# A third seven-product pair in an FFN input product, with its buffers, orders and jobs rearranged

## The chip, the cores and the metric

The kernel runs on one core of a Trainium2 chip. The metric is the device time of one execution in microseconds (us), the median of several runs. The engines of the core run side by side, each through its own queue in program order, and wait for each other by semaphores: TensorE (PE; its weight loads are PEld), VectorE (DVE), ScalarE (ACT), GpSimd (POOL) and SyncE (SP, which issues the DMAs).

## What is computed

A decoder trunk of two layers on 256 positions of width 2048, in float32. Each layer has a token mixer (layer 0: causal pooling with a 512x512 map per channel group; layer 1: sparse attention with an indexer), cross-attention to a memory of 256 rows with 4 heads, and a SwiGLU feed-forward network (FFN) of hidden width 5632, each on an RMS-normed input and added to x. A last RMSNorm follows.

```python
for i in range(DEPTH):
    h = rms_norm(x, norm_mix[i])
    x = x + (pool_mixer(h, ...) if i % 2 == 0 else dsa_attention(h, ...))
    x = x + memory_cross_attention(rms_norm(x, norm_xattn[i]), memn, ...)
    x = x + swiglu(rms_norm(x, norm_ffn[i]), ffn_w_in[i], ffn_w_out[i])
def swiglu(h, w_in, w_out):
    g, u = jnp.split(h @ w_in, 2, axis=-1)
    return (jax.nn.silu(g) * u) @ w_out
```

## The kernel before, in words

Every weight is read once, as a *piece* of 128 partitions x 2048 columns (1 MB), by a DMA of SyncE into one of three *raw* buffers. The products run in a reduced float format (fp32r), so each operand is split into a high part and a low rest, and one product is three matmuls of 512 columns: high x high, high x low, low x high. `high` (L151) is a copy on ACT, `low` (L154) a subtraction on DVE, `raw - high`. A plain piece is split in two *units* of 1024 columns (L157). High and low parts lie in buffers of a pool with tag "w": eight tiles of 2048 columns, two per plain piece.

The order on each engine is the order in which the program text issues the instructions, written by hand. `hook` (L243) is called after every few matmuls: it runs one due *job* (a function put aside with a delay in hooks), and issues one unit of splitting for a piece ahead, two where the lead is short. `split_unit` (L201) issues nothing where the tiles held, `state["held"]`, would pass `W_BUFS`. A piece's tiles are given back, in issue order, by `w_done` (L224); on the chip ACT then waits until TensorE's last matmul on that buffer is over.

The FFN's input product works on *chunks* `j` of 512 hidden columns, gate and up, eleven per layer (`chunk_in`, L725). Four accumulators of one PSUM bank each (2 halves of the rows x gate and up) are filled over eight *pairs* `kp` of k-tiles, one piece each. A plain pair takes eight products of 24 matmuls (`eight`). For the pairs in `SEVEN = (3, 5)`, taken as 2x2 blocks, seven products suffice, 21 matmuls (`seven`, L745): four are added to accumulators or intermediate sums `m` (two "sm" and two "tp" PSUM banks), and sums of weight blocks and of activation blocks are needed. The weight sums are made by DVE in `split_seven` (L169), in four steps s0 to s3; s0 fills the first pair of tiles (b), s1 to s3 the second (t). b is given back in the middle of the pair. The activation sums are made by `combine` (L371), called from the second of the two jobs that transpose and split a quarter of x (`Normed.chunk`, L442). When the last seven pair is over, DVE turns `m` into four parts (L777 to L782); at the chunk's end it adds the accumulators to them (L793), ACT and DVE apply silu and the product, and two jobs transpose the result ("spread", L799).

The chunks stand in groups: 0 to 4, then the output product ("fo") of hidden chunks 0 to 3; 5 to 8 and fo of 4 to 7; 9 and 10 and fo of 8 to 10. fo uses two of the same four accumulators for each of four output quarters. `tables` (L854) makes the rotary tables for layer 1; it stands between layer 0's cross-attention and its FFN.

The joint from cross-attention to FFN: each quarter `n` of x is finished by two adds on DVE (`add_to_x`, L472), and jobs then transpose it on TensorE and split it on ACT and DVE (L358, L360).

Of the kernel before, what the change touches and what calls it, by code (L numbers as in the profile page):

```python
# [12 lines left out]
F32 = mybir.dt.float32  # L13
# [7 lines left out]
P = 128  # L21
# [11 lines left out]
SEVEN = (3, 5)  # L33
# [19 lines left out]
RAW_BUFS, W_BUFS, BIG_BUFS, TMP_BUFS = 3, 8, 11, 7  # L53
# [3 lines left out]
def trunk_kernel(ctx: ExitStack, tc: tile.TileContext, a: dict, out: bass.AP):  # L57
# [73 lines left out]
    state = {"load": 0, "split": 0, "cur": 0, "hook": 0, "held": 0}  # L131
# [25 lines left out]
    def split_plain(i, t, w):  # L157

        def unit(c, first):
            def fn():  # L160
                if first:
                    parts[i] = (w_tile("wh"), w_tile("wl"))
# [3 lines left out]
            return 2 if first else 0, fn  # L166
        return [unit(slice(c, min(c + UNIT, w)), c == 0) for c in range(0, w, UNIT)]

    def split_seven(i, t):  # L169

        r = t.rearrange("p (s c) -> p s c", s=4)
        p = {}

        def s0():
            p["bh"], p["bl"] = w_tile("bh"), w_tile("bl")
            p["t"] = wpool.tile([P, 2, 512], F32, tag="t13", name="t13", bufs=1)
            parts[i] = p
            V.tensor_tensor(p["t"], r[:, 2:4, :], r[:, 0:1, :].to_broadcast([P, 2, 512]), op=ALU.add)
# [12 lines left out]

        def s3():
            low(p["tl"][:, 1024:2048], t[:, 0:1024], p["th"][:, 1024:2048])

        return [(2, s0), (2, s1), (0, s2), (0, s3)]

    def is_seven(i):
        key = pieces[i][0]
        return key[0] == "fi" and key[3] in SEVEN

    def split_unit(must=False):  # L201

        i = state["split"]
        if i >= len(pieces):
            return
        load_to(i + RAW_BUFS)
        if not steps:
            steps.extend(split_seven(i, raws[i][0]) if is_seven(i) else split_plain(i, *raws[i]))
        if state["held"] + steps[0][0] > W_BUFS:
            assert not must  # L210
            return
        steps.popleft()[1]()
        if not steps:
            raws.pop(i)
            state["split"] += 1
# [8 lines left out]
    def w_done(tiles=2):  # L224
        parts.pop(state["cur"])
        state["cur"] += 1
        state["held"] -= tiles
# [143 lines left out]
    def combine(tp, kt0, gi):  # L371

        s = work.tile([P, 1024], F32R, tag="sums", name="sums", bufs=2)
        f, c = tmp(), tmp()
        for u in range(2):
            A.activation(f[:, u * S:(u + 1) * S], tp[:, u * S:(u + 1) * S], AF.Copy, scale=gain(gi, kt0 + u))
        a11, a21, a12, a22 = (f[:, i * P:(i + 1) * P] for i in range(4))
# [56 lines left out]
    class Normed:  # L434
# [7 lines left out]
        def chunk(self, n, later=0):  # L442

            def pair(u):
# [4 lines left out]
                if kt0 // 2 in self.seven:  # L449
                    self.sums[kt0 // 2] = combine(tp, kt0, self.gi)  # L450
                sumsq(self.ss[:, u, n:n + 1], x[:, u, n * 512:(n + 1) * 512])

            job(lambda: pair(0), NORM_CHUNK[0] + later)
# [263 lines left out]
    def ffn(L, xn, nxt):  # L717
# [7 lines left out]
        def chunk_in(j):  # L725
# [6 lines left out]
            def eight(kp, w):  # L732
                wh, wl = w
                xt = xn(kp // 2)
                for f, t in ((0, 0), (0, 1), (1, 0), (1, 1)):
                    for u in range(2):
                        k = 2 * (kp % 2) + u
                        ws = c(((2, 0), (1, 3))[u][f])
# [6 lines left out]
            def seven(kp, w):  # L745
# [8 lines left out]
                last = kp == SEVEN[-1]  # L754
# [9 lines left out]
                three(acc[1], *s_(0), bh[:, c(2)], bl[:, c(2)], False, False)  # L764
# [3 lines left out]
                state["held"] -= 2  # L768
                three(acc[2], *a_(1, 1), w["th"][:, c(3)], w["tl"][:, c(3)], False, False)
                hook()  # L770
                for i, (p, si) in enumerate(((5, 2), (7, 3), (6, 1))):
                    three(m[p], *s_(si), w["th"][:, c(i)], w["tl"][:, c(i)], first, last)
                    if i == 1:
                        hook()
                w_done(2)
# [78 lines left out]
    def tables():  # L854
        posf = small.tile([P, 2], F32, tag="posf", name="posf")
        V.tensor_copy(posf, pos)
        ang, kk = (tmp(384).rearrange("p (c t f) -> p c t f", c=2, t=2) for _ in range(2))
# [14 lines left out]
        A.activation(kf, af, AF.Sin)  # L872
        sn, cs = kk[:, 0], kk[:, 1]
# [308 lines left out]
```

## Time and profile before

| | |
|---|---|
| time, three runs | 2001.17, 2001.29, 2003.45 us; median 2001.29 |
| profiled execution | 2002.29 us, its span 2000.5 us |
| mean granted TensorE clock | 0.993 of full |
| busy in the span | PE 1964.8, PEld 1630.6, DVE 1396.4, ACT 976.8, POOL 50.7 us |
| HBM read | 368.45 MB, 185 GB/s over the span |

The span is the time from the first to the last instruction; the execution's own time has some 1.8 us around it. Busy time is the time in which an engine worked. Matmuls overlap, so the time of one matmul in a stream is read from start to start and not from its duration. In the timeline, "x4" merges neighbours of the same kind into one line, and the brackets at the end give the idle time of the engine before the line and what ended it. L12 is line 12 of the kernel.

### The profile page before, as it was taken

To read this page: it belongs to the slowest core of one execution; us is meant where nothing else is said; L and a number is where in the kernel's file an instruction comes from. 1 tells how busy PE (TensorE), PEld (TensorE's weight loads), DVE (VectorE), ACT (ScalarE), POOL (GpSimd) and SP (SyncE) were. 2 spreads that over 40 slices of the span, in tenths; PEclk is the share of its full clock that TensorE was granted. 3 is DMA by queue.
4 is the path that set the end of the run, shared out by engine and by line. 5 is a ranking of instruction groups with operands and counts; after the bars stand their busy time and mean duration, and the time that the engine had idled before them with its cause. 6 is when DMAs were issued, how large, how long until landed. Compare 5 with 4: busy or idle time off the path is not lost.

```text
span 2000.5 us, 23131 instructions
## 1 busy us (share of the span) xinstructions
PE 1964.8 (98%) x9030; PEld 1630.6 (82%) x9030; DVE 1396.4 (70%) x1861; ACT 976.8 (49%) x1286; POOL 50.7 (3%) x97
## 2 busy tenths in 40 slices
PE   8999899999999999999999999899999999999997
PEld 7788788888888888888788888788888888888886
DVE  5765887874687756766777655778875578855774
ACT  6554654453454533544445554655553355533552
POOL 1200200000000000001000000100000000000000
PEclk9999999999999999999999999999999999999999
DMA  9445454565554554554444354355555455554552
GB/s 358 163 148 177 160 211 168 191 217 200 182 204 185 203 197 157 209 212 172 168 148 166 129 185 152 127 210 210 211 189 189 169 197 212 205 191 177 197 210 85
DMA packets 53679, 372.06 MB, mean 186 GB/s; under 512 B 6336, under 2 KB 6976, under 8 KB 9536
## 3 DMA queue, kind: packets, MB, share of 16 engines
q1 hardware_dynamic: 53136, 370.00, 51.3%
q8 instruction: 71, 1.16, 0.2%
q10 hardware_dynamic: 432, 0.57, 0.1%
q14 instruction: 40, 0.33, 0.0%
HBM read 368.45 MB, written 2.10 MB: 185 GB/s over the span
## 4 chain that ended last, share of the span: by engine, by line
PE 93%; DVE 2%; DMA 2%; ACT 1%; issue 1%; POOL 0%; ACTq 0%; DVEq 0%
PE acc L721 13%; PE acc L723 13%; PE acc L722 13%; PE acc L392 13%; PE acc L390 13%; PE acc L391 13%; PE acc L415 2%; PE acc L416 1%; PE tp L722 1%; PE sm L722 1%; PE tp L723 1%; PE sm L721 1%; PE tp L721 1%; PE sm L723 1%; PE tp L806 1%; DMA raw<-in_xv 1%
## 5 line engine op out<-in xcount | busy, mean ns | idle before, releaser
L155 DVE TENSOR_TENSOR wl<-raw,wh 128x1024 fp32r<-128x1024 f32 x600 | 708.0, 1217 | 318.8 <-ACT wh L152 317.5
L152 ACT ACTIVATE wh<-raw 128x1024 fp32r<-128x1024 f32 x600 | 604.6, 1048 | 501.6 <-PE acc L391 268.9
L390 PE MATMUL acc<-wh,big 128*128 128x512 f32 (+1 forms) x1184 | 476.5, 402 | 0.0
L392 PE MATMUL acc<-wh,big 128*128 128x512 f32 (+1 forms) x1184 | 460.2, 389 | 0.0
L391 PE MATMUL acc<-wl,big 128*128 128x512 f32 (+1 forms) x1184 | 459.3, 388 | 0.0
L721 PE MATMUL acc<-wh,big 128*128 128x512 f32 x1056 | 415.2, 393 | 0.0
L723 PE MATMUL acc<-wh,big 128*128 128x512 f32 x1056 | 412.0, 390 | 0.0
L722 PE MATMUL acc<-wl,big 128*128 128x512 f32 x1056 | 411.8, 390 | 0.0
L392 PEld LDWEIGHTS acc<-wh,big 128*128 128x128 f32 x1184 | 222.5, 188 | 46.4
L391 PEld LDWEIGHTS acc<-wl,big 128*128 128x128 f32 x1184 | 223.1, 188 | 43.6 <-issue 1.9
L390 PEld LDWEIGHTS acc<-wh,big 128*128 128x128 f32 x1184 | 222.8, 188 | 43.2 <-issue 1.9
L723 PEld LDWEIGHTS acc<-wh,big 128*128 128x128 f32 x1056 | 198.7, 188 | 41.6
L722 PEld LDWEIGHTS acc<-wl,big 128*128 128x128 f32 x1056 | 199.0, 188 | 40.2
L721 PEld LDWEIGHTS acc<-wh,big 128*128 128x128 f32 x1056 | 198.9, 188 | 40.2
L155 DVE TENSOR_TENSOR bl<-raw,bh 128x1536 fp32r<-128x1536 f32 x44 | 77.2, 1754 | 49.8 <-ACT bh L152 49.8
L152 ACT ACTIVATE bh<-raw 128x1536 fp32r<-128x1536 f32 x44 | 65.5, 1489 | 87.2 <-issue 68.6
L415 PE MATMUL acc<-big,wh 128*128 128x512 f32 x256 | 97.9, 421 | 5.3 <-ACT wh L152 4.6
L472 DVE TENSOR_TENSOR x<-acc,x 128x512 f32<-128x512 f32 x70 | 47.4, 690 | 46.2 <-PE acc L392 46.2
L351 ACT ACTIVATE big<-tp 128x512 fp32r<-128x512 f32 x44 | 26.4, 600 | 101.2 <-PE tp L806 101.2
L416 PE MATMUL acc<-big,wl 128*128 128x256 f32 x256 | 73.0, 285 | 0.5 <-DVE wl L155 0.5
L152 ACT ACTIVATE th<-raw 128x1024 fp32r<-128x1024 f32 x44 | 46.7, 1060 | 39.7 <-DVE raw L186 39.7
L415 PEld LDWEIGHTS acc<-big,wh 128*128 128x128 f32 x256 | 49.5, 193 | 18.2 <-ACT wh L152 4.9
(206 smaller groups left out, 1851.3 us busy)
## 6 DMA issues: line engine op xcount, KB each, us to landing
raw<-in_fi SPq DMA_DIRECT2D x176, 1024.0 KB, 4.8
raw<-in_fo SPq DMA_DIRECT2D x88, 1024.0 KB, 4.8
raw<-in_wq SPq DMA_DIRECT2D x16, 1024.0 KB, 4.8
raw<-in_wao SPq DMA_DIRECT2D x16, 1024.0 KB, 4.9
raw<-in_xv SPq DMA_DIRECT2D x8, 1024.0 KB, 7.0
raw<-in_xq SPq DMA_DIRECT2D x8, 1024.0 KB, 4.8
raw<-in_xo SPq DMA_DIRECT2D x8, 1024.0 KB, 4.8
raw<-in_wqi SPq DMA_DIRECT2D x8, 1024.0 KB, 5.0
```

The source lines that it names most:

```text
L152: A.activation(dst, src, AF.Copy)
L155: V.tensor_tensor(dst, src, hi.bitcast(F32), op=ALU.subtract)
L351: A.activation(dst_h, src, AF.Copy)
L390: T.matmul(acc[:, :w], lhsT=xh, rhs=wh[:, c0:c0 + w], start=first, stop=False)
L391: T.matmul(acc[:, :w], lhsT=xh, rhs=wl[:, c0:c0 + w], start=False, stop=False)
L392: T.matmul(acc[:, :w], lhsT=xl, rhs=wh[:, c0:c0 + w], start=False, stop=last)
L415: T.matmul(acc, lhsT=wh[:, c0:c0 + P], rhs=xt[:, k, :], start=first, stop=False)
L416: T.matmul(acc[:, S:2 * S], lhsT=wl[:, c0:c0 + P], rhs=xt[:, k, 0:S], start=False, stop=last)
L472: V.tensor_tensor(xc, acc[t], xc, op=ALU.add)
L721: T.matmul(acc, lhsT=xh, rhs=wh, start=first, stop=False)
L722: T.matmul(acc, lhsT=xh, rhs=wl, start=False, stop=False)
L723: T.matmul(acc, lhsT=xl, rhs=wh, start=False, stop=last)
```

## The change

The seven-product set becomes (1, 3, 5) in chunks 1 to 10 of each layer; chunk 0 keeps (3, 5). The pairs are taken in another order, 0, 2, 1, 4, 3, 6, 5, 7 (chunk 0: 0, 1, 2, 4, 3, 6, 5, 7), so that a plain pair stands between any two seven pairs and one plain pair behind the last. High and low parts share one buffer: four of twice the size in place of eight. The four weight blocks lie in another order in memory, and `split_seven` makes the sums in place in the raw buffer, without a tile of its own. Outside `chunk_in` the splitting may hold three buffers only (`W_SHORT`), inside it four. In `Normed.chunk` the scaled copies for the activation sums are made in the transposing job (`scaled`), and the sums themselves in a job of their own, one hook later. The rotary tables become two jobs in the first output product of layer 0.

```diff
-SEVEN = (3, 5)
+PAIRS, SEVEN = (0, 2, 1, 4, 3, 6, 5, 7), (1, 3, 5)
+PAIRS_FIRST, SEVEN_FIRST = (0, 1, 2, 4, 3, 6, 5, 7), (3, 5)
...
-RAW_BUFS, W_BUFS, BIG_BUFS, TMP_BUFS = 3, 8, 11, 7
+RAW_BUFS, W_BUFS, BIG_BUFS, TMP_BUFS = 3, 4, 11, 7
+W_SHORT = 3
...
-            for kp in range(8):
+            for kp in (PAIRS if j else PAIRS_FIRST):
                 plan(("fi", L, j, kp), a["fi"][L, j, kp])
...
-        return wpool.tile([P, 2048], F32R, tag="w", name=name, bufs=W_BUFS)
+        return wpool.tile([P, 2, 2048], F32R, tag="w", name=name, bufs=W_BUFS)
...
         def s0():
-            p["bh"], p["bl"] = w_tile("bh"), w_tile("bl")
-            p["t"] = wpool.tile([P, 2, 512], F32, tag="t13", name="t13", bufs=1)
+            b = w_tile("b")
+            p["bh"], p["bl"] = b[:, 0, :], b[:, 1, :]
             parts[i] = p
-            V.tensor_tensor(p["t"], r[:, 2:4, :], r[:, 0:1, :].to_broadcast([P, 2, 512]), op=ALU.add)
-            high(p["bh"][:, 0:1536], t[:, 512:2048])
-            low(p["bl"][:, 0:1536], t[:, 512:2048], p["bh"][:, 0:1536])
+            for c in (slice(0, 1024), slice(1536, 2048)):
+                high(p["bh"][:, c], t[:, c])
+                low(p["bl"][:, c], t[:, c], p["bh"][:, c])
 
         def s1():
-            p["th"], p["tl"] = w_tile("th"), w_tile("tl")
-            high(p["th"][:, 0:1024], p["t"].rearrange("p s c -> p (s c)"))
-            V.tensor_tensor(r[:, 0, :], p["t"][:, 0, :], r[:, 3, :], op=ALU.add)
-            V.tensor_tensor(r[:, 1, :], r[:, 0, :], r[:, 1, :], op=ALU.add)
+            b = w_tile("t")
+            p["th"], p["tl"] = b[:, 0, :], b[:, 1, :]
+            V.tensor_tensor(r[:, 1:3, :], r[:, 1:4:2, :], r[:, 2:3, :].to_broadcast([P, 2, 512]), op=ALU.add)
+            high(p["th"][:, 512:1536], t[:, 512:1536])
+            V.tensor_tensor(r[:, 3, :], r[:, 1, :], r[:, 3, :], op=ALU.add)
+            V.tensor_tensor(r[:, 0, :], r[:, 3, :], r[:, 0, :], op=ALU.add)
 
         def s2():
-            high(p["th"][:, 1024:2048], t[:, 0:1024])
-            low(p["tl"][:, 0:1024], p["t"].rearrange("p s c -> p (s c)"), p["th"][:, 0:1024])
+            for c in (slice(1536, 2048), slice(0, 512)):
+                high(p["th"][:, c], t[:, c])
+            low(p["tl"][:, 512:1536], t[:, 512:1536], p["th"][:, 512:1536])
 
         def s3():
-            low(p["tl"][:, 1024:2048], t[:, 0:1024], p["th"][:, 1024:2048])
-        return [(2, s0), (2, s1), (0, s2), (0, s3)]
+            for c in (slice(1536, 2048), slice(0, 512)):
+                low(p["tl"][:, c], t[:, c], p["th"][:, c])
+        return [(1, s0), (1, s1), (0, s2), (0, s3)]
...
-        if state["held"] + steps[0][0] > W_BUFS:
+        if state["held"] + steps[0][0] > (W_BUFS if must else state["cap"]):
...
                 if kt0 // 2 in self.seven:
-                    self.sums[kt0 // 2] = combine(tp, kt0, self.gi)
+                    f = scaled(tp, kt0, self.gi)
+                    late.append(lambda: self.sums.update({kt0 // 2: combine(f)}))
...
+            if {2 * n, 2 * n + 1} & set(self.seven):
+                job(sums, NORM_CHUNK[1] + 1 + later)
...
+            pairs, sevens = (PAIRS, SEVEN) if j else (PAIRS_FIRST, SEVEN_FIRST)
+            for kp in pairs:
...
+            state["cap"] = W_BUFS
             for j in range(t0 + (gi > 0), t1 + (not last)):
                 chunk_in(j)
+            state["cap"] = W_SHORT
+            for fn in between if gi == 0 else ():
+                job(fn, 6)
...
-    tables()
-    ffn(0, f0, m1)
+    ffn(0, f0, m1, tables())
```

## Rows read from the trace of the kernel before

**Rows 1.** The page, part 1: busy time of each engine

```profile
PE 1964.8 (98%) x9030; PEld 1630.6 (82%) x9030; DVE 1396.4 (70%) x1861; ACT 976.8 (49%) x1286; POOL 50.7 (3%) x97
```

**Rows 2.** Stages, one FFN chunk: stretch, length, busy PE, PEld, DVE, ACT, POOL, clock

```profile
297.48:340.57 43.09, 43.09 (x195) 35.70 (x194) 34.56 (x36) 22.09 (x23) 0.00 (x0) 1.00 0.54 195
```

**Rows 3.** TensorE's waits: who ended them; us in total, times, longest

```profile
PE tp L367 <- DVE x L472: 12.4, 2, 6.2
...
PE tp L585 <- DVE big L360: 3.2, 1, 3.2
...
PE tp L512 <- DVE tmp L506: 2.0, 1, 2.0
```

**Rows 4.** Timeline of TensorE, one chunk: start us, us, engine, line, operation

```profile
309.30 0.39 PE L721 MATMUL acc<-wh,big 128*128 128x512 f32 x1
...
340.57 0.39 PE L721 MATMUL acc<-wh,big 128*128 128x512 f32 x1
```

**Rows 5.** Timeline of VectorE, same chunk; in brackets idle time before, and releaser

```profile
310.41 2.36 DVE L155 TENSOR_TENSOR wl<-raw,wh 128x1024 fp32r<-128x1024 f32 x2 [1.34 <-ACT wh L152]
...
326.05 4.63 DVE L155 TENSOR_TENSOR wl<-raw,wh 128x1024 fp32r<-128x1024 f32 x4 [2.06 <-ACT wh L152]
...
330.60 0.68 DVE L779 TENSOR_TENSOR tmp<-tp,tmp 128x512 f32<-128x512 f32 x1
...
333.38 2.35 DVE L155 TENSOR_TENSOR wl<-raw,wh 128x1024 fp32r<-128x1024 f32 x2
...
338.48 1.88 DVE L793 TENSOR_TENSOR tmp<-acc,tmp 128x512 f32<-128x512 f32 x3
```

**Rows 6.** Timeline of ScalarE, same chunk

```profile
309.32 2.01 ACT L152 ACTIVATE wh<-raw 128x1024 fp32r<-128x1024 f32 x2 [2.02 <-PE acc L722]
...
330.20 2.01 ACT L152 ACTIVATE wh<-raw 128x1024 fp32r<-128x1024 f32 x2 [0.70 <-DMA raw<-in_fi]
```

**Rows 7.** The page, part 6: DMA issues, KB each, median us to landing

```profile
raw<-in_fi SPq DMA_DIRECT2D x176, 1024.0 KB, 4.8
```

**Rows 8.** Timeline of VectorE, first joint from cross-attention to FFN

```profile
201.05 0.29 DVE L379 TENSOR_TENSOR tmp<-tmp 128x128 f32<-128x128 f32 x1 [0.91 <-ACT tmp L376]
...
202.77 0.69 DVE L352 TENSOR_TENSOR sums<-tmp,sums 128x512 fp32r<-128x512 f32 x1 [0.70 <-ACT sums L351]
...
211.50 1.28 DVE L472 TENSOR_TENSOR x<-acc,x 128x512 f32<-128x512 f32 x2
```

**Rows 9.** Timeline of TensorE, after waits at the start and at the joint

```profile
68.23 0.48 PE L585 MATMUL tp<-big,x 128*128 128x144 f32 x2 [3.21 <-DVE big L360]
...
106.50 0.50 PE L415 MATMUL acc<-big,wh 128*128 128x512 f32 x1 [0.40 <-DVE big L360]
...
106.83 0.28 PE L416 MATMUL acc<-big,wl 128*128 128x256 f32 x1
...
212.24 1.50 PE L367 MATMUL tp<-ident,x 128*128 128x128 f32 x4 [6.21 <-DVE x L472]
...
213.96 0.63 PE L722 MATMUL acc<-wl,big 128*128 128x512 f32 x1
...
214.39 0.63 PE L723 MATMUL acc<-wh,big 128*128 128x512 f32 x1
```

**Rows 10.** Timeline of VectorE, the rotary tables: first and last operation

```profile
215.50 0.16 DVE L856 CAST posf<-pos 128x2 f32<-128x2 int32 x1
...
221.54 0.18 DVE L879 COPY big<-tmp 128x64 f32<-128x64 f32 x1
```

**Rows 11.** Timeline of VectorE, the first 60 us

```profile
38.79 1.23 DVE L155 TENSOR_TENSOR wl<-raw,wh 128x1024 fp32r<-128x1024 f32 x1 [4.64 <-ACT wh L152]
...
42.29 0.34 DVE L325 TENSOR_REDUCE rs<-ss 128x1 f32<-128x4 f32 x2
...
50.61 0.48 DVE L506 TENSOR_SCALAR tmp<-ident,memr 128x128 f32<-128x128 f32 x2 [1.51 <-POOL memr L341]
...
56.40 0.52 DVE L518 TENSOR_SCALAR big<-big,rs 128x576 f32<-128x576 f32 x1 [3.42 <-POOL rs L341]
```

More of the change, by code (lines that the diff above doesn't have):

```diff
@@ L129, in trunk_kernel @@
                     plan(("fo", L, ht, n), a["fo"][L, ht, n])
-    state = {"load": 0, "split": 0, "cur": 0, "hook": 0, "held": 0}
+    state = {"load": 0, "split": 0, "cur": 0, "hook": 0, "held": 0, "cap": W_SHORT}
     raws, parts, steps = {}, {}, deque()
@@ L161, in fn @@
                 if first:
-                    parts[i] = (w_tile("wh"), w_tile("wl"))
+                    w2 = w_tile("w")
+                    parts[i] = (w2[:, 0, :], w2[:, 1, :])
                 wh, wl = parts[i]
@@ L165, in fn @@
                 low(wl[:, c], t[:, c], wh[:, c])
-            return 2 if first else 0, fn
+            return 1 if first else 0, fn
         return [unit(slice(c, min(c + UNIT, w)), c == 0) for c in range(0, w, UNIT)]
@@ L222, in w_get, with w_done @@
         return parts[i]
-    def w_done(tiles=2):
+    def w_done():
         parts.pop(state["cur"])
         state["cur"] += 1
-        state["held"] -= tiles
+        state["held"] -= 1
     jobs, side = deque(), deque()
@@ L369, in transpose_pair, with scaled, combine @@
         return tp
-    def combine(tp, kt0, gi):
-        s = work.tile([P, 1024], F32R, tag="sums", name="sums", bufs=2)
-        f, c = tmp(), tmp()
+    def scaled(tp, kt0, gi):
+        f = tmp()
         for u in range(2):
             A.activation(f[:, u * S:(u + 1) * S], tp[:, u * S:(u + 1) * S], AF.Copy, scale=gain(gi, kt0 + u))
+        return f
+    def combine(f):
+        s = work.tile([P, 1024], F32R, tag="sums", name="sums", bufs=len(SEVEN))
+        c = tmp()
         a11, a21, a12, a22 = (f[:, i * P:(i + 1) * P] for i in range(4))
@@ L449, in pair, with sums @@
                 if kt0 // 2 in self.seven:
-                    self.sums[kt0 // 2] = combine(tp, kt0, self.gi)
+                    f = scaled(tp, kt0, self.gi)
+                    late.append(lambda: self.sums.update({kt0 // 2: combine(f)}))
                 sumsq(self.ss[:, u, n:n + 1], x[:, u, n * 512:(n + 1) * 512])
+            def sums():
+                for fn in late:
+                    fn()
+            late = []
             job(lambda: pair(0), NORM_CHUNK[0] + later)
             job(lambda: pair(1), NORM_CHUNK[1] + later, (self.name, n))
+            if {2 * n, 2 * n + 1} & set(self.seven):
+                job(sums, NORM_CHUNK[1] + 1 + later)
             if n == 3:
@@ L714, in cross, with ffn @@
             done(acc, n)
-    def ffn(L, xn, nxt):
+    def ffn(L, xn, nxt, between=()):
         hs = {}
@@ L737, in eight @@
                         k = 2 * (kp % 2) + u
-                        ws = c(((2, 0), (1, 3))[u][f])
+                        ws = c(((1, 2), (0, 3))[u][f])
                         three(acc[2 * t + f], xt[:, k, t * P:(t + 1) * P], xt[:, k, S + t * P:S + (t + 1) * P],
@@ L753, in seven @@
                     first = False
-                last = kp == SEVEN[-1]
+                last = kp == sevens[-1]
                 def a_(t, u):
@@ L763, in seven @@
                 bh, bl = w["bh"], w["bl"]
-                three(acc[1], *s_(0), bh[:, c(2)], bl[:, c(2)], False, False)
+                three(acc[1], *s_(0), bh[:, c(3)], bl[:, c(3)], False, False)
                 three(acc[0], *a_(0, 1), bh[:, c(0)], bl[:, c(0)], False, False)
@@ L767, in seven @@
                 three(m[1], *a_(0, 0), bh[:, c(1)], bl[:, c(1)], first, last)
-                state["held"] -= 2
-                three(acc[2], *a_(1, 1), w["th"][:, c(3)], w["tl"][:, c(3)], False, False)
+                state["held"] -= 1
+                three(acc[2], *a_(1, 1), w["th"][:, c(0)], w["tl"][:, c(0)], False, False)
                 hook()
                 for i, (p, si) in enumerate(((5, 2), (7, 3), (6, 1))):
-                    three(m[p], *s_(si), w["th"][:, c(i)], w["tl"][:, c(i)], first, last)
+                    three(m[p], *s_(si), w["th"][:, c(i + 1)], w["tl"][:, c(i + 1)], first, last)
                     if i == 1:
                         hook()
-                w_done(2)
+                w_done()
                 if last:
@@ L783, in seven @@
                     m["part"] = (v, e, u, d)
-            for kp in range(8):
+            pairs, sevens = (PAIRS, SEVEN) if j else (PAIRS_FIRST, SEVEN_FIRST)
+            for kp in pairs:
                 w = w_get(("fi", L, j, kp))
-                (seven if kp in SEVEN else eight)(kp, w)
+                (seven if kp in sevens else eight)(kp, w)
                 if kp < 7:
@@ L854, in tables, with angles @@
     def tables():
+        k = []
+        return [lambda: k.append(angles()), lambda: spread_tables(k[0])]
+    def angles():
+        ang, kk = (tmp(384).rearrange("p (c t f) -> p c t f", c=2, t=2) for _ in range(2))
         posf = small.tile([P, 2], F32, tag="posf", name="posf")
         V.tensor_copy(posf, pos)
-        ang, kk = (tmp(384).rearrange("p (c t f) -> p c t f", c=2, t=2) for _ in range(2))
         for t in range(2):
@@ L872, in tables, with spread_tables @@
         A.activation(kf, af, AF.Sin)
+        return kk
+    def spread_tables(kk):
         sn, cs = kk[:, 0], kk[:, 1]
@@ L1143 @@
     win = i["attn_w_in"][0]
-    fi = [w.reshape(8, 2, P, 2, HT, 512).transpose(4, 0, 2, 1, 3, 5).reshape(HT, 8, P, 4, 512)[:, :, :, [1, 2, 0, 3]]
+    fi = [w.reshape(8, 2, P, 2, HT, 512).transpose(4, 0, 2, 1, 3, 5).reshape(HT, 8, P, 4, 512)[:, :, :, [2, 0, 1, 3]]
           .reshape(HT, 8, P, 2048) for w in i["ffn_w_in"]]
```

2 lines of the change are left out of this document (1 added, 1 removed).

## The prediction

> **What bounds the kernel now.** I read the page's busy shares first: TensorE is busy 98% of the span [rows 1]. Then the busy time by stage: in one chunk of the FFN's input product, from 297.48 to 340.57 us, TensorE is busy all 43.09 us, VectorE 34.56 and ScalarE 22.09 [rows 2]. The list of TensorE's own waits shows where it stands still: not in the FFN loops, but at the two joints from cross-attention to FFN (6.2 us each) and a few times before 107 us [rows 3]. So a matmul less in a chunk is time saved only while VectorE (DVE) and ScalarE (ACT) keep pace, and the question is whether they do, not on the mean but at the tightest place.
>
> The matmul's price: between the start of pair 2's first matmul at 309.30 and the next chunk's first at 340.57 lie 138 matmuls (4 pairs of 24, 2 of 21) [rows 4]: 31.27 / 138 = 0.2266 us each. A chunk of 186 takes 42.15; the rest of 43.09, two times 0.47, are the transposes of the chunk before.
>
> **Part 1, the third seven-product pair.** It saves 3 matmuls in each of the 10 later chunks of both layers: 60 x 0.2266 = 13.6 us. The chunk becomes 42.41 us.
>
> Its price on DVE, start to start: a 1024-column subtraction costs 1.137 (four lows from 326.05 end where the next operation starts, 330.60), an independent 512-column operation 0.60 (three adds in 1.88), one that reads the result before it 0.72 (330.60 to the end of the four at 333.38 is 2.78) [rows 5]. A plain pair is 2.27. The new seven pair: b part 1.137 + 0.60; sums 1.14 + 0.72 + 0.72; lows 1.137 + 0.60 + 0.60; about 6.65. Five plain pairs, three seven, the m part 2.78, four adds and two products at the chunk's end 3.7, two spreads 1.2: 39 of 42.41 us. On the mean DVE still has 3 us to spare.
>
> The mean is not the limit, since the four weight buffers tie DVE to TensorE. The order in a chunk is 0, 2, 1\*, 4, 3\*, 6, 5\*, 7 (\* = seven). I count who holds a buffer when the next pair's first is taken: while pair 5\* (two buffers) and 7 (one) are pending, the only free one is pair 6's. So the next chunk's pair 0 cannot be split before TensorE has ended pair 6. After that, TensorE has pairs 5\* and 7 left: 45 x 0.2266 = 10.20 us. DVE must in the same time do, in its own order:
> - wait for ACT: 0.02 from the pair's end to ACT (309.30 to 309.32) and 1.09 from there to DVE's low (310.41) [rows 4 to 6]: 1.11
> - next pair 0: 2.275; next pair 2: 2.275, and 0.26 before it, for its load. A raw buffer is free when DVE ends pair 5\*, which by the same walk (pair 5\* starts 1.11 after pair 4's end) is 2.35 us before pair 6's end; the load lands 4.8 us after issue [rows 7], a case that the trace has already (ACT waits 0.70 for a load) [rows 6]
> - the m part of pair 5\*, now one pair from the end and no longer two: 2.78
> - the b part of the next chunk's pair 1\*: 1.737
> - the first add of the chunk's end: 0.68, and 0.05 to TensorE (211.50 + 0.68 to 212.24) [rows 8, 9]
>
> Sum 11.17. All four acc banks are in use, so the next chunk's first matmul waits for that add, and TensorE's whole queue stands behind it: 11.17 - 10.20 = 0.97 us at each passage from chunk to chunk. Before, the same place had slack: the adds started at 338.48, two us ahead of 340.57 [rows 4, 5]. Where an output product follows (three times a layer), DVE has a whole plain pair in place of the b part (+0.54), and the second accumulator's add comes third (0.52 more): 2.03. Per layer 8 x 0.97 + 3 x 2.03; for both 27.7 us. Bounds for one passage: 0.7 if the load is in time, 1.25 if each handover costs 0.05 more; 22 to 34 us in all.
>
> The Trainium skill (VectorE: DVE Perf Modes, the section on the TRN2 errata) prices an fp32 tensor_tensor at (N+151)/0.96 ns, an estimate of 1.22 and 0.69 us here, and caps it at one element a cycle, so that sums in place are no cheaper. The rows agree with the duration of one (0.68 for 512 columns); start to start they are shorter (four of 1024 in 4.63). By the page's price the passages would cost about 40 us and the kernel would take some 2019.
>
> **Part 2, weight sums in place, one buffer for high and low.** Same columns on DVE, four more instructions per seven pair; counted above. ACT has 20 us to spare in a chunk [rows 2]: nothing.
>
> **Part 3, activation sums as jobs.** At the joint, TensorE waits for the transposes of x's last quarter, behind DVE's add at 211.50 to 212.24 [rows 8, 9]. Ahead of that add stood two inline combines, in each of which DVE waited 0.91 for ACT [rows 8]. As jobs, one of the pair splits moves behind the add and that wait goes; a third combine comes in (four small sums, 1.0, and a 512 low, 0.6, with 0.7 for ACT [rows 8]). Walking DVE's queue from 187.6 with these gives the first add's end at 210.4, 1.8 earlier. Two joints: -3.6 us (bounds 0 and -5).
>
> **Part 4, rotary tables moved.** DVE spends 215.50 to 221.7 on them [rows 10], under TensorE's first pairs, where TensorE doesn't wait [rows 3]. In the output product DVE needs 2.27 of each 5.44 us, so they are hidden again; their one ACT table load too. 0; without that cover 6 us.
>
> **Part 5, shorter lead elsewhere.** Three buffers in place of four take one pair (5.44 us) off the lead. Elsewhere no TensorE wait for weights is listed but at the start [rows 3], so I take 0 there. At the start there is a gain: DVE's and ACT's queues stood 4.64 us behind a weight load (until 38.79), and the sums for mem's norm came after it (42.29), then GpSimd, then mem_diag at 50.61, then x's norm, 56.40, then the diffs at 68.23 [rows 9, 11]. With one pair less ahead, the mem sums come in front of that load, near 35.5; x's norm then starts near 46.6 and not 52.1, TensorE's 2.0 us wait goes, and the diff that it waited 3.2 us for starts near 62.8. I take -5 us, bounds -7 and 0 (DMA order in the first 50 us shifts too).
>
> **Sum**: -13.6 + 27.7 - 3.6 - 5 = +5.5 us. The profiled execution took 2002.29 us (span 2000.5, 1.8 around it), the median is 2001.29; added to the median: **2006.8**.
>
> **Rivals.**
> *TensorE stays the bound*: the mean (39 of 42.41) decides, and the adds are never late. It needs DVE's 11.17 us to be under 10.20. For it: 3 us of spare DVE time, and no wait there before. Against: the idle time lies ahead of pair 6's end, where no buffer is free to use it. Then 2001.3 - 13.6 - 8.6 = 1979; faster. Halfway, with waits of half the size: 1993.
> *The clock falls at the passages*: after waits of 2.0, 3.2 and 6.2 us matmuls ran at 0.43 us a piece (213.96 to 214.39, the 1.2 GHz level) for about six matmuls, 1.2 us lost [rows 3, 9]; after 0.4 us they didn't (106.50 to 106.83) [rows 9]. My waits, 1 to 2 us, lie between. If each of the 22 passages cost that, +26: 2033; if only the six long ones, 2014.
> The Trainium skill (TensorE: Matmul & The Clock Gate, the section on a second HAM failure mode) describes this: short idles between matmul groups as PSUM banks are cycled, and a clock that swings. By that rule this rival would hold; the trace shows falls only from 2.0 us up.
> *The start gets no better*, since the new order of loads delays a weight as much as it advances the norm: 2011.8, part of the forecast's range.
>
> **How the numbers follow.** Forecast 0.70, clock 0.08, TensorE-bound 0.13, halfway 0.09. 0.2% (4 us) is about what a measurement of this kernel tells from no change. In the forecast's case the bounds (22 to 34, 0 to -7, 0 to -5) put about 0.50 over 2005.3, 0.18 within 0.2% and 0.02 below; halfway is split. Faster 0.19, same 0.23, slower 0.58. The range 1993 to 2014 leaves out the TensorE-bound case and most of the clock's.
>
> **What would show it.** A new entry in TensorE's waits: acc's first matmul of a chunk or of the output product on DVE's add at the chunk's end, some 22 times, near 1 us (2 in the output product). The chunk's period 43.4 and not 42.4. DVE's order ahead of that add: pair 0, pair 2, four m operations, the b part, with no idle but the 1.1 us behind pair 6's end. The joint's wait near 4.4 and not 6.2; no wait at mem_row; the diff's wait near 63. I am wrong if the chunks repeat at 42.4, if the adds run ahead of the chunk's end, or if the granted clock falls in the FFN.

## The result, and the profile after

The changed kernel takes 2020.0 us (2019.55 to 2021.02), the kernel before on the same chip 2002.4: ratio 1.0085, 95% interval 1.0070 to 1.0100. The forecast was 2006.8 (1993 to 2014), so the sign was right and the time fell outside the range. The profiled execution has a span of 2018.1 us, 17.6 more than before.

The page's first part, which answers [rows 1]: the engines' busy time, its share, the instructions.

```profile
PE 1955.2 (97%) x8970; PEld 1615.3 (80%) x8970; DVE 1486.5 (74%) x2079; ACT 1007.3 (50%) x1439; POOL 46.0 (2%) x97
```

60 matmuls are gone as meant; TensorE is busy 9.6 us less and the span is 17.6 us longer, so TensorE stands still some 27 us more. One chunk of the input product, as in [rows 2] (stretch, length, busy PE, PEld, DVE, ACT, POOL, clock):

```profile
294.74:338.55 43.81, 42.69 (x191) 35.05 (x192) 39.09 (x47) 23.65 (x31) 0.00 (x0) 1.00 0.52 192
```

It repeats every 43.8 us (before 43.09, forecast 43.4), with 1.1 us in which TensorE does nothing, and a full clock. TensorE's waits, as in [rows 3] (what waited, who ended it: us in total, times, longest):

```profile
PE acc L743 <- DVE tmp L816: 19.2, 16, 2.3
PE acc L404 <- DVE tmp L816: 9.9, 6, 1.7
PE tp L377 <- DVE big L370: 6.1, 2, 3.1
PE tp L377 <- DVE x L494: 5.8, 3, 3.2
...
PE tp L607 <- DVE big L370: 2.3, 1, 2.3
```

The first two lines are new: 16 passages from chunk to chunk and 6 to the output product, 29.1 us, each ended by DVE's add at the chunk's end (L816). The joints' waits have changed their places, not their size: 11.9 us behind two instructions of DVE, 12.4 before. The wait at mem_row (L512 of the kernel before) is gone and the one at the diffs (L607, before L585) is 2.3 for 3.2.

One passage on three engines; TensorE first, at the end of pair 6 and at the end of the chunk (start, length, line, out<-in, idle before it):

```profile
326.85 0.39 PE L745 MATMUL acc<-w,big 128*128 128x512 f32 x1
327.07 0.39 PE L743 MATMUL acc<-b,sums 128*128 128x512 f32 x1
...
337.05 0.39 PE L745 MATMUL acc<-w,big 128*128 128x512 f32 x1
338.55 0.47 PE L743 MATMUL acc<-w,big 128*128 128x512 f32 x1 [1.12 <-DVE tmp L816]
338.86 0.39 PE L744 MATMUL acc<-w,big 128*128 128x512 f32 x1
```

ScalarE takes the freed buffer for the next pair 0, then one for pair 2. The profile names no releaser for the first ("issue"); that it is the buffer is read from the time, 0.25 us after pair 6's end, and from the run n_sep below:

```profile
327.32 2.01 ACT L156 ACTIVATE w<-raw 128x1024 fp32r<-128x1024 f32 x2 [2.03 <-issue]
329.84 2.01 ACT L156 ACTIVATE w<-raw 128x1024 fp32r<-128x1024 f32 x2 [0.51 <-DMA raw<-in_fi]
```

VectorE, the list that I had written out in Part 1, in the forecast's order:

```profile
328.42 2.36 DVE L159 TENSOR_TENSOR w<-raw,w 128x1024 fp32r<-128x1024 f32 x2 [1.17 <-ACT w L156]
330.93 2.36 DVE L159 TENSOR_TENSOR w<-raw,w 128x1024 fp32r<-128x1024 f32 x2 [0.15 <-ACT w L156]
333.21 0.68 DVE L801 TENSOR_TENSOR tmp<-tp,tmp 128x512 f32<-128x512 f32 x1
...
335.99 1.82 DVE L159 TENSOR_TENSOR b<-raw,b 128x1024 fp32r<-128x1024 f32 x2
337.72 2.48 DVE L816 TENSOR_TENSOR tmp<-acc,tmp 128x512 f32<-128x512 f32 x4
```

Pair 6 ends at 327.07, where pair 5's first matmul starts. From there to TensorE's restart at 338.55 are 11.48 us (forecast 11.17); TensorE's own work in that time is 45 matmuls, 10.21 us. The difference, 1.27, is the wait.

### The profile page after: what moved, and what is told of

Its sections match the earlier page's. It is cut to its first block, busy times and chain, and to the rows that moved or that the text cites. A ratio compares the mean times of both kernels' runs of the same rounds, so it can differ in the third digit from the quotient of the medians.

```text
span 2018.1 us, 23360 instructions
## 1 busy us (share of the span) xinstructions
PE 1955.2 (97%) x8970; PEld 1615.3 (80%) x8970; DVE 1486.5 (74%) x2079; ACT 1007.3 (50%) x1439; POOL 46.0 (2%) x97
## 4 chain that ended last, share of the span: by engine, by line
PE 67%; DVE 16%; issue 6%; DMA 5%; ACT 5%; ACTq 0%; DVEq 0%
PE acc L404 13%; PE acc L406 13%; PE acc L405 13%; PE acc L743 6%; PE acc L744 5%; PE acc L745 5%; DMA raw<-in_fi 4%; DVE w L159 4%; ACT w L156 3%; PE acc L429 3%; DVE b L159 3%; DVE t L159 2%; DMA raw<-in_fo 1%; PE acc L430 1%; DVE raw L191 1%
## 5 line engine op out<-in xcount | busy, mean ns | idle before, releaser
L159 DVE TENSOR_TENSOR w<-raw,w 128x1024 fp32r<-128x1024 f32 (+1 forms) x560 | 661.7, 1217 | 153.9 <-ACT w L156 151.9
L156 ACT ACTIVATE w<-raw 128x1024 fp32r<-128x1024 f32 (+1 forms) x560 | 563.9, 1047 | 266.3 <-PE acc L406 184.7
L404 PE MATMUL acc<-w,big 128*128 128x512 f32 (+1 forms) x1184 | 477.1, 403 | 9.9 <-DVE tmp L816 9.9
L406 PE MATMUL acc<-w,big 128*128 128x512 f32 (+1 forms) x1184 | 460.4, 389 | 0.0
L405 PE MATMUL acc<-w,big 128*128 128x512 f32 (+1 forms) x1184 | 459.6, 388 | 0.0
L743 PE MATMUL acc<-w,big 128*128 128x512 f32 x896 | 354.6, 396 | 19.2 <-DVE tmp L816 19.2
L745 PE MATMUL acc<-w,big 128*128 128x512 f32 x896 | 349.9, 391 | 0.0
L744 PE MATMUL acc<-w,big 128*128 128x512 f32 x896 | 349.9, 391 | 0.0
L404 PEld LDWEIGHTS acc<-w,big 128*128 128x128 f32 x1184 | 222.8, 188 | 55.4 <-issue 14.2
L406 PEld LDWEIGHTS acc<-w,big 128*128 128x128 f32 x1184 | 222.6, 188 | 46.6
L405 PEld LDWEIGHTS acc<-w,big 128*128 128x128 f32 x1184 | 223.2, 189 | 43.2 <-issue 1.9
L156 ACT ACTIVATE t<-raw 128x512 fp32r<-128x512 f32 (+1 forms) x192 | 134.5, 764 | 193.3 <-DVE raw L191 193.3
L743 PEld LDWEIGHTS acc<-w,big 128*128 128x128 f32 x896 | 169.0, 189 | 59.0 <-issue 25.5
L745 PEld LDWEIGHTS acc<-w,big 128*128 128x128 f32 x896 | 168.7, 188 | 35.7
L744 PEld LDWEIGHTS acc<-w,big 128*128 128x128 f32 x896 | 169.0, 189 | 33.4
L159 DVE TENSOR_TENSOR b<-raw,b 128x1024 fp32r<-128x1024 f32 (+1 forms) x128 | 116.7, 953 | 63.8 <-ACT b L156 63.8
L156 ACT ACTIVATE b<-raw 128x1024 fp32r<-128x1024 f32 (+1 forms) x128 | 101.2, 838 | 113.5 <-issue 97.1
L159 DVE TENSOR_TENSOR t<-raw,t 128x512 fp32r<-128x512 f32 (+1 forms) x192 | 155.1, 863 | 0.0
L429 PE MATMUL acc<-big,w 128*128 128x512 f32 x256 | 96.3, 415 | 6.2 <-ACT w L156 5.5
(203 smaller groups left out, 2026.3 us busy)
```

The source lines that it names most:

```text
L156: A.activation(dst, src, AF.Copy)
L159: V.tensor_tensor(dst, src, hi.bitcast(F32), op=ALU.subtract)
L404: T.matmul(acc[:, :w], lhsT=xh, rhs=wh[:, c0:c0 + w], start=first, stop=False)
L405: T.matmul(acc[:, :w], lhsT=xh, rhs=wl[:, c0:c0 + w], start=False, stop=False)
L406: T.matmul(acc[:, :w], lhsT=xl, rhs=wh[:, c0:c0 + w], start=False, stop=last)
L429: T.matmul(acc, lhsT=wh[:, c0:c0 + P], rhs=xt[:, k, :], start=first, stop=False)
```

## Experiments

Two theories stand against each other. *The path*: no buffer is free before pair 6 ends, so VectorE's list from there to the add decides, not its total. *The load*: VectorE with 39 us of work in 42.4 is simply too full. Times are medians in us; the ratio is to the kernel before, run beside it.

| run | what | time | ratio, 95% interval |
|---|---|---|---|
| n_two | two seven pairs, new order kept | 2042.9 | 1.0203 (1.0188 to 1.0219) |
| n_hold | no split between the m part and the chunk's products | 1985.0 | 0.9913 (0.9898 to 0.9927) |
| n_nat | three seven pairs, natural order | 2010.6 | 1.0038 (1.0024 to 1.0052) |
| n_sep | separate high and low tiles | 2015.6 | 1.0066 (1.0049 to 1.0082) |
| n_ffirst | scaled copies first | 2012.3 | 1.0049 (1.0034 to 1.0064) |
| n_inline | sums not as jobs | 2026.3 | 1.0116 (1.0100 to 1.0131) |
| n_cap4 | full lead everywhere | 2027.6 | 1.0125 (1.0109 to 1.0140) |
| b_short | before, shorter lead alone | 1999.2 | 0.9978 (0.9969 to 0.9988) |
| b_short_tab | the same, tables moved | 1996.4 | 0.9964 (0.9951 to 0.9977) |
| n_tab | tables not moved | 2026.8 | 1.0116 (1.0101 to 1.0131) |
| n_best | n_hold, n_sep, n_ffirst together | 1977.0 | 0.9871 (0.9857 to 0.9886) |
| n_natbest | natural order, n_sep, n_ffirst | 1999.9 | 0.9984 (0.9975 to 0.9994) |

### The passages: path or load

**n_two**

```diff
-PAIRS, SEVEN = (0, 2, 1, 4, 3, 6, 5, 7), (1, 3, 5)
+PAIRS, SEVEN = (0, 2, 1, 4, 3, 6, 5, 7), (3, 5)
```

> The changed kernel with only two seven-product pairs, (3, 5), in every chunk; its order of pairs, its buffers and its jobs stay. The path theory (between pair 6's end and the chunk's end VectorE has a fixed list, since no buffer is free earlier) says that the waits at the passages stay, although VectorE has 4.4 us less to do in a chunk: the list then has a whole plain pair in place of the b part, 2.275 for 1.737, so the wait from chunk to chunk grows from 1.28 to about 1.8 us and the 6 passages to the output product stay near 1.9. Time 2020 + 13.6 (60 more matmuls) + 16 x 0.54 - 2 (a third combine less at two joints) = about 2040 us. The rival, that VectorE's total of 39 in 42.4 us is what binds, says that with 34.6 of 43.1 the waits go: 2020 + 13.6 - 34 = about 2000 us.

Measured 2042.9. TensorE's waits:

```profile
PE acc L743 <- DVE tmp L816: 29.3, 16, 3.1
PE acc L404 <- DVE tmp L816: 10.6, 6, 1.9
```

VectorE has less to do (1402.2 us busy, about 84 less than with three pairs) and TensorE waits more. That rules the load out. It also tells that the dear part of the change is the order and the buffers, taken together; the third seven pair makes up for some of it, since only its b part stands on the path.

**n_hold**

```diff
...
-        if i >= len(pieces):
+        if i >= len(pieces) or (state["hold"] and not must):
             return
...
                     m["part"] = (v, e, u, d)
+                    state["hold"] = True
...
             h = (c12, c22)
+            state["hold"] = False
```

> The changed kernel, but between the m part of the last seven pair and the products at the chunk's end no weight split is issued; the splits that stood there (the b part of the next chunk's pair 1, or a plain piece of the output product) come right behind them. Nothing is left out, and VectorE's total stays the same. The path theory: the measured path of about 11.5 us loses 1.74, and 9.75 is less than TensorE's 10.2 us, so the 16 waits from chunk to chunk (1.375 us each) go; at the 6 passages to the output product (1.93 each) the second accumulator's add makes it about even, 0 to 0.3 us left. Time 2020 - 33 = about 1987 us, chunks repeating at 42.4. The rival, total load of VectorE: the same work in the same chunk, so the waits only change their place: 2018 to 2022 us. A third way: the b part is now late for pair 1, and TensorE waits there instead, 1 us or more in each chunk: about 2005 us.

Measured 1985.0, and not one wait on the chunk's add is left. VectorE around the same passage, and a chunk:

```profile
328.26 2.36 DVE L159 TENSOR_TENSOR w<-raw,w 128x1024 fp32r<-128x1024 f32 x2 [0.23 <-ACT w L156]
...
332.71 0.69 DVE L804 TENSOR_TENSOR tmp<-sm,tmp 128x512 f32<-128x512 f32 x1
333.32 2.48 DVE L817 TENSOR_TENSOR tmp<-acc,tmp 128x512 f32<-128x512 f32 x4
335.71 1.40 DVE L820 SCALAR_TENSOR_TENSOR tmp<-tmp,rs 128x512 f32<-128x512 f32 x2
337.03 1.82 DVE L159 TENSOR_TENSOR b<-raw,b 128x1024 fp32r<-128x1024 f32 x2
```

```profile
249.68:292.10 42.42, 42.42 (x192) 35.15 (x191) 39.10 (x47) 24.68 (x32) 0.00 (x0) 1.00 0.52 197
```

The b part now stands behind the adds and the products. VectorE does the same 39.1 us in a chunk, TensorE is busy all of its 42.42 us, and pair 1, taken third, isn't late. The 22 waits were worth 35 us, and they came from the place of 1.7 to 2.3 us of work, not from its amount.

**n_nat**

```diff
-PAIRS, SEVEN = (0, 2, 1, 4, 3, 6, 5, 7), (1, 3, 5)
+PAIRS, SEVEN = (0, 1, 2, 3, 4, 5, 6, 7), (1, 3, 5)
```

> The changed kernel with its three seven pairs (1, 3, 5), buffers and jobs, but in chunks 1 to 10 the pairs are taken in natural order 0 to 7, so that two plain pairs stand behind the last seven pair. The path theory: the next chunk's pair 0 then takes the buffer that pair 5 gives back in its middle, and the only work tied to pair 6's end is the t part of the next pair 1, about 3.7 us on VectorE, which with the add ends near 4.4 us, against TensorE's 5.4 us for pair 7. So 20 of the 22 waits go (the two of chunk 0, whose order is not changed, stay): 2020 - 31 = about 1989 us. If three seven pairs cost the waits whatever their order, since VectorE has 39 us to do in 42.4, 2015 to 2025 us.

Measured 2010.6: my expectation failed. The six waits ahead of the output product are gone, but the 16 others are still there. The two at the end of chunk 0 have grown to 3.9 us each, and the 14 others have fallen to some 0.7 from 1.1:

```profile
PE acc L743 <- DVE tmp L816: 17.6, 16, 3.9
```

```profile
327.63 2.36 DVE L159 TENSOR_TENSOR w<-raw,w 128x1024 fp32r<-128x1024 f32 x2 [1.17 <-ACT w L156]
330.34 2.36 DVE L159 TENSOR_TENSOR w<-raw,w 128x1024 fp32r<-128x1024 f32 x2 [0.35 <-ACT w L156]
...
335.39 1.81 DVE L159 TENSOR_TENSOR b<-raw,b 128x1024 fp32r<-128x1024 f32 x2
...
339.71 2.42 DVE L159 TENSOR_TENSOR t<-raw,t 128x1024 fp32r<-128x1024 f32 x3
342.05 2.48 DVE L816 TENSOR_TENSOR tmp<-acc,tmp 128x512 f32<-128x512 f32 x4
```

I had let the t part begin with an empty queue at pair 6's end. In truth the list hangs on an earlier release, the end of pair 4: pair 7 (327.63), pair 0, the m part, b and t of pair 1, and no idle but 0.35. From 327.63 to the first add's end (342.73) are 15.1 us, with 1.34 ahead of them 16.4, against 15.6 for TensorE's 69 matmuls. So the path again, but started one release earlier; where the list starts has to be read off, not assumed. The two waits of chunk 0 were not taken apart.

### The handover

**n_sep**

```diff
-        return wpool.tile([P, 2, 2048], F32R, tag="w", name=name, bufs=W_BUFS)
+        return [wpool.tile([P, 2048], F32R, tag="w", name=name + c, bufs=2 * W_BUFS) for c in "hl"]
...
```

> The changed kernel with the high and the low part of a weight in two tiles again, as before the change (eight tiles of 2048 columns, given back in pairs); order, sums in place and jobs stay. If the merged buffer is part of the miss, ScalarE's high at a passage starts after the last matmul but one on the old buffer, one matmul (0.23 us) earlier: the 22 waits shrink by 0.23 each, 5 us in all, 2015 us, and ScalarE starts some 0.02 after pair 6's end and not 0.25. If the merging costs nothing, as I had taken it, 2020 us and the same waits of 1.28.

Measured 2015.6. The last matmuls of pair 6 and the first of pair 5 on TensorE, and ScalarE's high:

```profile
325.31 0.39 PE L744 MATMUL acc<-wl,big 128*128 128x512 f32 x1
325.54 0.39 PE L745 MATMUL acc<-wh,big 128*128 128x512 f32 x1
325.77 0.39 PE L743 MATMUL acc<-bh,sums 128*128 128x512 f32 x1
```

```profile
325.79 2.01 ACT L156 ACTIVATE wh<-raw 128x1024 fp32r<-128x1024 f32 x2 [2.03 <-issue]
```

ScalarE starts 0.09 after the end of the last matmul but one (325.31 + 0.39), which is the last that reads the low tile. In the changed kernel it starts 0.08 after the end of the last matmul of all (326.85 + 0.39, and 327.32), since that one reads the high half of the same buffer. So a passage begins one matmul later with the merged buffer. In the trace of before, too, the releaser named at a pair's end is the last matmul but one (L722) [rows 6]. The median time at a passage from the last matmul's start to the next one's fell from 1.51 to 1.33 us (chunk to chunk) and from 2.05 to 1.81 (to the output product). The times alone, 2015.6 and 2020.0, don't settle it, since the intervals of the two ratios overlap; the rows do. One passage, at the end of chunk 0 of layer 1, had a longer wait, and there the clock fell to the 1.2 GHz level for some matmuls (0.43 us apart):

```profile
1323.00:1330.00 7.00, 6.96 (x24) 5.58 (x25) 6.60 (x9) 4.69 (x6) 0.00 (x0) 0.76 0.00 0
```

```profile
1323.04 0.47 PE L743 MATMUL acc<-wh,big 128*128 128x512 f32 x1 [2.22 <-DVE tmp L816]
```

### The joints

**n_ffirst** (in `transpose_pair`, with `copy` set for the seven pairs; `pair` no longer calls `scaled` itself)

```diff
...
+        f = scaled(tp, kt0, gi) if copy else None
         split_pair(dst, tp, kt0, gi)
-        return tp
+        return f
...
```

> The changed kernel, but at the joints ScalarE makes the scaled copies for the activation sums ahead of the high parts of the same transposes, and no longer behind VectorE's low parts. If ScalarE's stand of 1.4 to 1.65 us on VectorE's low parts (three times a joint), and VectorE's 2.5 us behind the next weight high that follows from it, are what ate the expected gain of the joints, the joint gets 1.5 to 3 us shorter each and the time is about 2015 us (2014 to 2017). If the joint is bound by what VectorE has to do there in all (three combines), nothing changes: 2019 to 2021 us.

**n_inline**

```diff
-                    late.append(lambda: self.sums.update({kt0 // 2: combine(f)}))
+                    self.sums[kt0 // 2] = combine(f)
...
-            if {2 * n, 2 * n + 1} & set(self.seven):
-                job(sums, NORM_CHUNK[1] + 1 + later)
```

> The changed kernel with the activation sums made inside the transposing job again, right behind the scaled copies; only the jobs are undone. My record had the jobs as worth 3.6 us over two joints (one split moves ahead of the add, 0.91 us of wait goes in each). If so, about 2023 to 2025 us. If the jobs bring nothing, since ScalarE's scaled copy waits for VectorE's low parts either way, 2019 to 2021 us. If they cost, as each puts the wait of 0.7 us for the high part of the sums in front of the next add, under 2018 us.

Measured 2012.3 and 2026.3, the first below and the second above what I had expected. What VectorE does at the joint is read as the time from its first add of x's quarter 0 to that of quarter 3 (rows of `add_to_x`). This time does not follow the clock: in the changed kernel the granted clock is 0.93 of full over the first joint and 0.99 over the second, and the lengths are 25.03 and 25.09 us.

| kernel | sums at the joint | first joint | second joint |
|---|---|---|---|
| before | two, inline | 23.90 | 23.91 |
| n_inline | three, inline | 27.80 | 27.87 |
| after | three, as jobs | 25.03 | 25.09 |
| n_two | two, as jobs | 21.68 | 21.68 |
| n_ffirst | three, as jobs, copies first | 21.80 | 21.81 |

The first joint of before, from here to 211.50 [rows 8], and then that of the changed kernel:

```profile
187.60 1.37 DVE L472 TENSOR_TENSOR x<-acc,x 128x512 f32<-128x512 f32 x2 [4.81 <-PE acc L392]
```

```profile
181.84 1.37 DVE L494 TENSOR_TENSOR x<-acc,x 128x512 f32<-128x512 f32 x2 [4.81 <-PE acc L406]
...
206.87 1.28 DVE L494 TENSOR_TENSOR x<-acc,x 128x512 f32<-128x512 f32 x2
```

n_best has 21.8 too. The jobs bring 2.8 us a joint (n_inline to after), and the third sum costs 3.4 (n_two to after). With the copies first, three sums take as long as two with the copies behind (21.80 and 21.68); two sums with the copies first were not run. Of the changed kernel, the second joint, ScalarE and then VectorE:

```profile
1262.79 0.83 ACT L368 ACTIVATE big<-tp,gains 128x256 fp32r<-128x256 f32 x2
1265.04 0.84 ACT L384 ACTIVATE tmp<-tp,gains 128x256 f32<-128x256 f32 x2 [1.41 <-DVE big L370]
...
1266.38 1.05 ACT L156 ACTIVATE w<-raw 128x1024 fp32r<-128x1024 f32 x1
```

```profile
1264.07 0.87 DVE L370 SCALAR_TENSOR_TENSOR big<-tp,gains,big 128x256 fp32r<-128x256 f32 x2
1267.47 1.23 DVE L159 TENSOR_TENSOR w<-raw,w 128x1024 fp32r<-128x1024 f32 x1 [2.52 <-ACT w L156]
```

The scaled copy reads the same PSUM bank as VectorE's low part and starts only when that has ended (1264.94, the copy 1265.04); the next weight high is queued behind it, and VectorE stands 2.52 us for that high. With the copies first, VectorE's same wait is 0.68:

```profile
1263.39 1.23 DVE L159 TENSOR_TENSOR w<-raw,w 128x1024 fp32r<-128x1024 f32 x1 [0.68 <-ACT w L156]
```

The Trainium skill (PSUM — Partial Sum Buffer, Terms) says that two engines at one bank at once collide, reads against reads included. The trace has the two readers of one bank one after the other, 0.10 us apart, and the copy waits there for a semaphore that VectorE's low part sets. So it is the program that keeps them apart; what an overlap would do, no run here shows.

### Lead and rotary tables

**n_cap4**

```diff
-W_SHORT = 3
+W_SHORT = 4
```

> The changed kernel with four buffers outside the FFN's input product too, in place of three: the shorter lead alone is undone. If the gain of 5.8 us ahead of 250 us comes from the shorter lead (VectorE's and ScalarE's queues no longer stand behind a weight load ahead of mem's norm), TensorE's wait at mem_row and the later one at the diffs come back and the time is about 2026 us. If it came from another part of the change, 2020 us.

**b_short**

```diff
...
-        if state["held"] + steps[0][0] > W_BUFS:
+        if state["held"] + steps[0][0] > (W_BUFS if must else state["cap"]):
...
+            state["cap"] = W_BUFS
             for j in range(t0 + (gi > 0), t1 + (not last)):
                 chunk_in(j)
+            state["cap"] = 6
```

> The kernel before with one edit: outside the FFN's input product it may hold six weight tiles, not eight. If the start's gain is the shorter lead's alone, about 2002 - 5.8 = 1996.5 us, all of it ahead of 110 us. If the shorter lead costs waits for weights elsewhere (output products, attention) that the change's buffers hide, 1998 to 2004 us. If it brings nothing without the rest, 2002 us.

**b_short_tab** has besides `tables` as a job in the first output product:

> The kernel before with the shorter lead outside the FFN's input product and the rotary tables as a job in the first output product. The shorter lead alone gave 1999.2: ahead of the joint it gained 6.4 us, and 3.4 were lost at the end of chunk 0, where VectorE came 2.8 us late with its adds. If the tables' 6.2 us on VectorE, in that chunk, are what made it late, that wait goes and the time is about 1996 us (1995 to 1997). If the shorter lead alone made it late, 1999 us again.

**n_tab**

```diff
-    ffn(0, f0, m1, tables())
+    for fn in tables():
+        fn()
+    ffn(0, f0, m1)
```

> The changed kernel with the rotary tables back ahead of layer 0's FFN; only that part is undone. My record had the move as worth nothing. If the tables are hidden there, 2019 to 2021 us. If with the shorter lead VectorE's 6.2 us for them come out at the end of chunk 0, where the adds are already 2.4 us late, the wait there grows by 2 to 6 us: 2022 to 2026 us.

n_cap4 took 2027.6. Its wait at mem_row is back, `PE tp L534 <- DVE tmp L528: 3.2, 1, 3.2`, and TensorE is 5.8 us later from 70 us on: the start's gain is the shorter lead's. b_short had it too (6.4 us by 72 us) but ended only 3.7 ahead, for a reason at the end of chunk 0:

```profile
PE acc L721 <- DVE tmp L793: 2.8, 1, 2.8
```

```profile
250.94 0.76 PE L721 MATMUL acc<-wh,big 128*128 128x512 f32 x1 [2.78 <-DVE tmp L793]
251.50 0.63 PE L722 MATMUL acc<-wl,big 128*128 128x512 f32 x1
251.93 0.63 PE L723 MATMUL acc<-wh,big 128*128 128x512 f32 x1
```

Behind that wait 13 matmuls ran at 0.43 us from start to start. (The traced execution, 2002.3 us, is the slowest of the ten; their median is 1999.2.) With the tables moved the wait is gone and the time 1996.4, as expected. n_tab, 2026.8, is the same seen from the other side. The standstill at the end of chunk 0 grows from 2.4 to 4.4 us beyond a matmul's usual time, TensorE waits for a weight near 220 us (1.2 and 0.8), and the clock falls after both. So with the shorter lead the tables' 6.2 us on VectorE are no longer hidden ahead of the FFN: it took their cover away, and the move gives it back.

### Putting it together

**n_best**

> The three edits of the runs n_hold, n_sep and n_ffirst together. If what they remove lies in different places (passages, joints), hold-back and early copies add up: 1985.0 - (2020.0 - 2012.3) = about 1977 us; separate tiles bring nearly nothing more, since the passages that they shortened have no wait left (0 to -1). If the joint's gain in n_ffirst came only because the chunks behind it had waits to absorb it, the sum is smaller, 1980 to 1985 us.

Measured 1977.0, 1.3% less than the kernel before. In this trace the clock stays at full over both joints (1.00 from 190 to 220 us, 0.89 in before), so part of the gain is the clock's. The longest waits that are left:

```profile
PE acc L430 <- ACT wh L156: 5.2, 1, 5.2
PE tp L377 <- DVE x L495: 5.1, 4, 2.3
PE tp L377 <- DVE big L370: 3.1, 2, 1.6
PE tp L608 <- DVE big L370: 2.3, 1, 2.3
```

**n_natbest**

> Natural order in chunks 1 to 10, high and low parts in separate tiles, early copies at the joints; no hold-back. If the three do what they did by themselves: 1989 - 7.7 (joints) - 0.5 (the two chunk-0 passages) = about 1981 us, against 1977 for hold-back with the change's order. If natural order leaves VectorE late inside the chunks (pair 1 wanted second, not third), 1985 us or more, with waits for weights inside the chunks.

Measured 1999.9, not 1981: the expectation rested on that of n_nat and falls with it; 15.1 us of waits on the chunk's add remain.

## Why the prediction was right and wrong

| term | recorded | measured in the changed kernel |
|---|---|---|
| 60 matmuls | -13.6 | -13.6 (a chunk without waits takes 42.42 in n_hold, 42.41 recorded) |
| 16 passages chunk to chunk | +15.5 | +23.0 (21.7 of standstill, and 0.08 each as the first matmul takes longer) |
| 6 passages to the output product | +12.2 | +11.3 (10.85 and 6 x 0.08) |
| two joints | -3.6 | +2.3 between VectorE's adds; +1.8 on TensorE |
| start | -5 | -5.8 |
| sum | +5.5 | +17.2, with the joints as TensorE has them +16.7; the span says +17.6 |

Of the forecast's miss of 13.2 us, the passages make 6.6 (Parts 1 and 2), the joints 5.4 (Part 3) and the base 1.1: the kernel before, run again, has a median of 2002.4 and not 2001.3. The start came out 0.8 better than forecast.

The joints' +1.8 comes from setting the start of every matmul of the two traces side by side: TensorE leaves the first joint 0.1 us better than before and the second 1.9 worse, while VectorE's last add comes 1.1 us later in the first and 1.2 in the second. At the first joint the clock makes the difference: behind the last wait it is full (1.00 from 207.6 to 214 us), where before it was 0.51 (212.24 to 215.5). Kernels with the same joint differ there by up to 2.6 us (+1.0 for both joints in the trace of n_sep, +3.5 in that of n_hold), so a saving of 1 us at a joint can't be read from one execution's time.

**Part 1**, the mechanism, was right: 22 waits, on that add, at those places, in that order of VectorE's list, and for the reason given (n_two, n_hold). VectorE's steps, from start to start, hold to 0.03 us: pair 0 with the load 2.51 (2.535 recorded), pair 2 2.28, the m part 2.78, the b part 1.73, TensorE's rest 10.21 (10.20). Mis-sized was the term for one passage, 0.97 where it is 1.35 (1.27 and the pitch), by the handovers from engine to engine: pair 6's end to ScalarE took 0.25 and not 0.02, the add's end (338.40) to TensorE 0.15 and not 0.05, and the first matmul after a standstill has a pitch (its start to the next one's) of 0.31 and not 0.23. The first I had from [rows 4, 6], where the tiles were still separate, the second from a transpose at a joint [rows 8, 9]; the third I had no row for and left out. My upper bound of 1.25 was too tight for the same reason. The passage at the end of chunk 0 is 1.26 in layer 1, like the rest, but 2.41 in layer 0; why stays open.

**Part 2** stands with "nothing" in the record, and that step failed; it makes the first of these three handovers: the merged buffer costs about 0.2 us at each passage (0.18 and 0.24 by the medians), 4 us in all (n_sep). I had only counted its columns, not when it comes free.

**Part 3** had the largest error of a single term: 5.9 us on VectorE, where it was forecast. That the jobs help is right (2.8 us a joint). But my 1.8 had the third sum in it, at a price of 2.3; if all of that stood ahead of the add, two sums would come out 4.1 us shorter, and n_two shows 2.2. So the gain of the jobs was put too high as well. The main failing step is "a third combine comes in (four small sums, 1.0, and a 512 low, 0.6, with 0.7 for ACT)": I priced its own instructions, 2.3 us, and not that ScalarE's scaled copy waits for VectorE's low parts with the next weight high queued behind it. The third sum costs 3.4 us a joint, and putting the copies first takes 3.2 of them back (n_ffirst). The trace of before had shown that wait already, on ScalarE at the first joint:

```profile
200.18 0.84 ACT L376 ACTIVATE tmp<-tp,gains 128x256 f32<-128x256 f32 x2 [1.99 <-DVE big L360]
```

**Part 4**, 0 for the tables, holds between the two kernels, in both of which they are hidden, but not for the move itself: with the shorter lead they are no longer hidden where they stood (n_tab), and in the changed kernel the move is worth 6.8 us. The two parts belong together, which I had not seen. **Part 5** was right, -5.8 for -5, and it is the shorter lead (n_cap4).

**Rivals.** TensorE bound by the mean (1979) falls with the 22 waits and with n_two. It named the right quantity for another kernel, though: n_hold, in which the path is short enough, is TensorE-bound in the FFN, at 1985. The clock rival (2033): in the changed kernel's trace the clock fell at none of the 22 passages. The Trainium skill (TensorE: Matmul & The Clock Gate, A second HAM failure mode) has the clock swing with short idles between groups. The traces here show no swing, but single falls after waits of 2.22 us (n_sep), 2.78 (b_short) and at 3 of n_two's 22 (1.85, 1.92 and 3.12), while one of 2.00 in n_two and this one of the changed kernel brought none:

```profile
250.94 0.47 PE L743 MATMUL acc<-w,big 128*128 128x512 f32 x1 [2.26 <-DVE tmp L816]
```

So the length of one wait doesn't settle it. By the price of the Trainium skill (VectorE: DVE Perf Modes, The TRN2 errata), the kernel would have taken 2019, the prediction's estimate. That is next to what was measured, but not for that reason: start to start VectorE's steps are those of the rows of before, and the missing time lies in handovers and joints.

## What to carry to other kernels

When few buffers tie a helper engine to the bound one, follow the helper's queue from the release of a buffer to the instruction that the bound engine waits for; what stands between counts in full, however idle that engine is on the mean, and work that isn't wanted yet belongs behind that instruction (35 us here for holding back some 2 us of it at each of 22 places). Price each handover from a row where the same two engines wait for each other, and when tiles are merged ask when the merged one comes free. Where the program lets two engines read one PSUM bank only one after the other, as here, put first the reader with the longer queue behind it.

## What the hardware showed unexpectedly

A second reader of a PSUM bank waited for the first, 1.41 us on ScalarE, though neither writes it; the wait is on a semaphore, so it is the program's order and not shown to be the chip's. A matmul that TensorE waited for starts 0.15 us after VectorE's add has ended and has a pitch of 0.31 us; in a stream it is 0.227. After waits of 1.9 to 4.3 us in the FFN the granted clock sometimes fell to the 1.2 GHz level, for 5 to 13 matmuls at 0.43 us (0.76 over 7 us in n_sep), and sometimes didn't.
